# A two-layer hybrid decoder on one core: copies of late weights queued behind other ScalarE work, and a convolution spread over 25 weight units

## The chip, the core and the metric

The kernel runs on one core of a Trainium2 chip. TensorE (PE) multiplies, VectorE (DVE) and ScalarE (ACT) do elementwise work, GpSimd (POOL) here only raises a variance to the power -1/2, and SyncE (SP) issues the weight loads. The metric is the device time of one execution in microseconds, the median of the runs. The weight loads of PE, which overlap its matmuls, are called PEld.

## What is computed

Two layers over 256 rows of 1024 columns, all in fp32. Cut to what matters:

```python
for l in range(DEPTH):                                  # DEPTH = 2
    u = x * (1.0 + sc1) + sh1                           # sc, sh, gt: from c @ w_ada[l] + b_ada[l]
    proj = u @ w_in[l]                                  # q, k, v | GLU input | two gates
    attn = softmax(rope(q) @ rope(k).T / 8, causal) @ v # 8 heads of 64
    h = a * sigmoid(g)                                  # (a, g) = GLU input
    h = depthwise_conv(h, 31 taps) + b                  # along the 256 rows
    conv = silu(layer_norm(h))
    y = (sigmoid(g1) * (attn @ w_attn_br) + sigmoid(g2) * (conv @ w_conv_pw)) @ w_out
    x = layer_norm(ALPHA * x + (1.0 + gt1) * y)
    u = x * (1.0 + sc2) + sh2
    x = layer_norm(ALPHA * x + (1.0 + gt2) * (square(relu(u @ w_up)) @ w_down))
```

## The kernel before

Every fp32 matrix is split into a high part and a low part, and a product is three matmuls: high by high, high by low, low by high (`rowmm`, L317; `colmm`, L323). Weights come as 232 **units** of 128x1024 numbers in the order in which PE uses them. `Stream.make` (L114) does a unit: SP loads the raw unit `w`, ACT copies it into the high part `wh` (L122), DVE subtracts to get the low part `wl` (L123). The raw ring has 5 buffers, the split ring `RING` = 8: unit n+8 can be copied only after PE's last matmul on unit n. Units 0 to 115 belong to layer 1, 116 to 231 to layer 2. Of layer 2: 116 to 123 are the GLU input, 124 to 131 q and k, 132 to 135 v, 136 to 151 the gates (four groups g of four units), 152 to 155 the attention branch, 156 to 159 the convolution branch, 160 to 167 the output projection, 168 to 175 the first part of `w_up`.

A scheduler turns the program into one fixed queue per engine, and each engine takes its queue in that order. Beside PE's main stream, generators are advanced a step at each unit (`bg.step()`), so that their work falls between units: `conv_steps` (L595) yields `CONV_GAP[l]` units after each of its 60 tap steps; `attn_steps` (L647) runs scores (tile `s`), exponentials (`P`, L683, with sums `sm`), the scaling of `P` by 1/sum (L690), transposes (`ptr`, `PT`) and values (`av`, then `ah` and `al`) for four pairs of heads; `rope_steps` (L732) transposes q and k and copies them (`qT`, `kT`, L736); `ada_dve_gate` (L489) and `ada_dve_cols` (L463) accumulate the modulation on DVE (tile `adaa`).

At the end of each sub-layer the rows are normed in halves h = 0 and 1: `norm_half` (L547) on DVE (`ygt`, `xall`, `st`, `ag`, `ve`, then POOL's `rstd`, then `xall` again), and `make_u` (L526) per half and per c = 0, 1: PE transposes `xall` (tile `utr`), ACT makes `uf` (L535) and its high part `u` (L537), DVE its low part `u` (L538). The next sub-layer's matmuls read both parts of `u`. The convolution ends in `conv_steps` from L621: PE transposes `acc` (`ctr`), DVE norms (`cst`, `cag`, `ve`, `cn`), PE transposes back (`cbk`), ACT makes `cz`, a tanh and the high part `ch` (L643), DVE the low part `cl` (L644), per half. Units 156 to 159 multiply by `ch` and `cl`.

```python
a = nc.scalar.activation(wh, w, AF.Copy)                              # L122
b = nc.vector.tensor_tensor(wl, w, wh.bitcast(F32), op=ALU.subtract)  # L123
```

`order(later, earlier)` (L309) fixes that one instruction stands behind another in its engine's queue, without a wait.

Of the kernel before, what the change touches and what calls it, by code (L numbers as in the profile page):

```python
# [14 lines left out]
AF = mybir.ActivationFunctionType  # L15
# [10 lines left out]
HD = 64  # L26
# [8 lines left out]
RAW = 5  # L35
ADA_MIX = 2.0
ADA_BUFS = 3
CONV_GAP = (0.35, 0.35)
FIRST_AHEAD = 1
FIRST_ORDER = 8  # L40
FIRST_MM = 6
# [25 lines left out]
H = [slice(0, 128), slice(128, 256)]  # L67
# [33 lines left out]
class Stream:  # L101
# [3 lines left out]
    def __init__(self, nc, raw, split, units, order):  # L105
        self.nc, self.raw, self.split, self.units, self.order = nc, raw, split, units, order
        self.behind = ()
        self.splits = []
        self.after = None
        self.live = {}  # L110
        self.made = 0
        self.taken = 0

    def make(self):  # L114
        nc = self.nc
        src = self.units[self.made]
        w = self.raw.tile([128, 1024], F32, name=f"w{self.made}", tag="raw")
        v = w if len(src.shape) == 2 else w.rearrange("p (k n) -> p k n", k=src.shape[1])
        nc.sync.dma_start(v, src)
        wh = self.split.tile([128, 1024], F32R, name=f"wh{self.made}", tag="wh")  # L120
        wl = self.split.tile([128, 1024], F32R, name=f"wl{self.made}", tag="wl")
        a = nc.scalar.activation(wh, w, AF.Copy)  # L122
        b = nc.vector.tensor_tensor(wl, w, wh.bitcast(F32), op=ALU.subtract)  # L123
        for i, j in zip((a, b), self.behind):
            self.order(i, j)
        self.behind = ()
        if self.after is not None:
            self.order(b, self.after)
        self.splits.append(b)
        self.live[self.made] = (wh, wl)  # L130
        self.made += 1

# [21 lines left out]
def trunk_kernel(ctx: ExitStack, tc: tile.TileContext, x_in, c_in, positions, w_in, w_attn_br,  # L154
                 conv_dw_w, conv_dw_b, conv_ln_g, conv_ln_b, w_conv_pw, w_out, w_ada, b_ada,
                 ln_mix_g, ln_mix_b, w_up, w_down, ln_ffn_g, ln_ffn_b, out):
    nc = tc.nc
# [151 lines left out]
    def order(later, earlier):  # L309

        tc.add_manual_dep(later.ins, earlier.ins.name,
                          mybir.DependencyInfo(mybir.DependencyClass.NoSync, mybir.DependencyReason.DATA), reason="order")

    ws = Stream(nc, raw_p, split_p, units, order)
# [211 lines left out]
    def make_u(u, h, G, B, at):  # L526
        uh, ul, _ = u
        for c in range(2):
            ts = []
            b = transpose4(xt[h][:, 512 * c:512 * c + 512], "utr", ts)  # L530
            place(ts, at)
            f = t_p.tile([128, 4, 128], F32, name="uf", tag="t")
            for i in range(4):
                k = 4 * c + i
                nc.scalar.activation(f[:, i, :], b[:, 128 * i:128 * i + 128], AF.Identity, scale=G[:, k:k + 1], bias=B[:, k:k + 1])  # L535
            hi = uh[:, h, 4 * c:4 * c + 4, :]
            nc.scalar.activation(hi, f, AF.Copy)  # L537
            made_u[0] = nc.vector.tensor_tensor(ul[:, h, 4 * c:4 * c + 4, :], f, hi.bitcast(F32), op=ALU.subtract)  # L538

    def rstd_of(var, name):  # L540
        ve = s_p.tile([128, 1], F32, name="ve", tag="ve")
# [105 lines left out]
    def attn_steps(l, qkT, vs, hold):  # L647

        qT, kT = qkT
        ah = c_p.tile([128, 4, S], F32R, name="ah", tag="c")  # L650
        al = c_p.tile([128, 4, S], F32R, name="al", tag="c")
        hold["attn"] = (ah, al)
        sbs, Ps, sms, mxs, PTs = {}, {}, {}, {}, {}
        parts = (slice(0, 128), slice(128, 384))

        def scores(p):
            sb = []
            for e in range(2):
                es = slice(64 * e, 64 * e + 64)
                b = bank(f"s{e}")  # L660
                sb.append(b)
                nc.tensor.matmul(b[:, 0:128], qT[es, p, 0:128], kT[es, p, 0:128], start=True, stop=False, skip_group_check=True)
                nc.tensor.matmul(b[:, 128:384], qT[es, p, 128:256], kT[es, p, :], start=False, stop=False, skip_group_check=True)
            for e in range(2):
                nc.tensor.matmul(sb[e][:, 0:128], identb, maskb, start=False, stop=True, skip_group_check=True)
                nc.tensor.matmul(sb[e][:, 256:384], identb, maskb, start=False, stop=True, skip_group_check=True)
            mx = s_p.tile([128, 4], F32, name="mx", tag="mx")
            with tc.high_priority(MAX_PRIO):
                for e in range(2):
                    for i in range(2):  # L670
                        nc.vector.tensor_reduce(mx[:, 2 * e + i:2 * e + i + 1], sb[e][:, parts[i]], axis=AX.X, op=ALU.min)
            sbs[p], mxs[p] = sb, mx

        def exps(p):
            sm = s_p.tile([128, 4], F32, name="sm", tag="sm")
            Ps[p] = []
            for e in range(2):
                t = t_p.tile([128, 384], F32, name="P", tag="t")
                Ps[p].append(t)
                for i in range(2):  # L680
                    n = 2 * e + i
                    with tc.high_priority(EXP_PRIO):
                        nc.scalar.activation(t[:, parts[i]], sbs[p][e][:, parts[i]], AF.Exp, bias=mxs[p][:, n:n + 1],  # L683
                                             scale=-1.0, accum_out=sm[:, n:n + 1])
            with tc.high_priority(MAX_PRIO):
                nc.vector.reciprocal(sm, sm)
            for e in range(2):
                for i in range(2):
                    n = 2 * e + i
                    nc.scalar.activation(Ps[p][e][:, parts[i]], Ps[p][e][:, parts[i]], AF.Copy, scale=sm[:, n:n + 1])  # L690

        def transposes(p):
            PTs[p] = []
            for e in range(2):
                b = bank("ptr", tr)
                for i in range(3):
                    nc.tensor.transpose(b[:, 128 * i:128 * i + 128], Ps[p][e][:, 128 * i:128 * i + 128], ident)
                t = t_p.tile([128, 384], F32, name="PT", tag="t")
                with tc.high_priority(PT_PRIO):
                    nc.scalar.activation(t, b[:, 0:384], AF.Copy)  # L700
                PTs[p].append(t)

        def values(p):
            o = bank("av", tr)
            for e in range(2):
                es = slice(64 * e, 64 * e + 64)
                hs = slice((2 * p + e) * 64, (2 * p + e) * 64 + 64)
                nc.tensor.matmul(o[es, 0:256], vs[:, 0, hs], PTs[p][e][:, 0:256], start=True, stop=False, skip_group_check=True)
                nc.tensor.matmul(o[es, 128:256], vs[:, 1, hs], PTs[p][e][:, 256:384], start=False, stop=True, skip_group_check=True)
            hi = ah[:, p, :]  # L710
            nc.scalar.activation(hi, o[:, 0:256], AF.Copy)
            nc.vector.tensor_tensor(al[:, p, :], o[:, 0:256], hi.bitcast(F32), op=ALU.subtract)

        stages = (scores, exps, transposes, values)
        offs = ATTN_AT[l]
        for n in range(4 + offs[-1]):
            for k in reversed(range(len(stages))):
                if 0 <= n - offs[k] < 4:
                    stages[k](n - offs[k])
            yield ATTN_GAP[l]  # L720
# [11 lines left out]
    def rope_steps(l, qkt, qkT):  # L732
        for c in range(2):
            for h in range(2):
                b = transpose4(qkt[h][:, 512 * c:512 * c + 512], "qktr")
                nc.scalar.activation(qkT[c][:, :, H[h]], b.rearrange("p (q t) -> p q t", q=4), AF.Copy,  # L736
                                     scale=1.0 if c else -(HD ** -0.5))
            yield ROPE_GAP[l]

    def glu_gate(h, c, a, g):  # L740
# [257 lines left out]
    def relu2(src):  # L998
        r = t_p.tile([128, 512], F32, name="relu", tag="t")
        nc.scalar.activation(r, src, AF.Relu)  # L1000
        q = t_p.tile([128, 512], F32, name="relusq", tag="t")
        nc.scalar.activation(q, r, AF.Square)
        return q

    def relu2_wide(banks, hh, hl):

# [9 lines left out]
    def ffn(l, u):  # L1016
# [10 lines left out]
        for h in range(2):  # L1027
            b = [bank("u0"), bank("u1")]
            row_phase(ids, h, lhs, b, release=h == 1)
            for c in range(2):  # L1030
                q = relu2(b[c])
                ts = []
                tb = transpose4(q, "htr", ts).rearrange("p (f t) -> p f t", f=4)
                place(ts, HTR_AT[h][c])
                hh, hl = hid[c]
                nc.scalar.activation(hh[:, h], tb, AF.Copy)
                nc.vector.tensor_tensor(hl[:, h], tb, hh[:, h].bitcast(F32), op=ALU.subtract)
# [222 lines left out]
```

## Time and profile before

| | |
|---|---|
| time, median of 3 runs | 754.68 us (752.5 to 756.81) |
| the profiled execution's own time | 754.61 us |
| its span, first to last instruction | 752.5 us |
| busy: PE, PEld | 730.7 us (97%), 613.8 us (82%) |
| busy: DVE, ACT, POOL | 623.0 us (83%), 437.3 us (58%), 13.2 us (2%) |
| mean granted clock of PE | 0.995 of full speed |

Of the profiled execution's time 2.1 us lie outside its span. The end of a matmul is modelled, so busy time of PE says little; the distance from one matmul's start to the next says whether PE ran or waited. In the lists of waits a row names who waited for whom, with the sum, the count and the longest.

### The profile page before, as it was taken

Reading aid. Unit: us, or ns where it says so; the run is one execution under the profiler, and the core shown is the slowest. Engines: PE = TensorE matmul, PEld = TensorE weight load, DVE = VectorE, ACT = ScalarE, POOL = GpSimd, SP = SyncE. Lnnn points to the kernel's source line nnn. Section 1 sums busy time; section 2 is a strip of 40 time slices with the busy share of each in tenths; the row PEclk is TensorE's granted clock in tenths of the full one; section 3 lists DMA queues with packets and bytes.
Section 4 is the critical chain, followed back from the end, with each engine's and each line's share of the span. In section 5 each row is a group of like instructions: output and inputs, shape, how many; then the busy total and the mean of one; then the engine's idle time right before and its main releaser. Section 6 shows DMA issues by size and latency. Waiting matters only on the chain. (4 is left out here: it accounts for less than half of the span.)

```text
span 752.5 us, 11535 instructions
## 1 busy us (share of the span) xinstructions
PE 730.7 (97%) x4264; PEld 613.8 (82%) x4264; DVE 623.0 (83%) x942; ACT 437.3 (58%) x737; POOL 13.2 (2%) x37
## 2 busy tenths in 40 slices
PE   6999999999999999999999999999999999999995
PEld 4667788899888888888877888899988788888885
DVE  3448999999799999899899899998869895666657
ACT  4449898875575554544354875976447555454430
POOL 0000000010000000000000000001000000000001
PEclk9999999999999999999999999999999999999999
DMA  9999988677368999999786745436547896555501
GB/s 287 316 324 315 317 312 314 225 248 251 114 246 290 371 382 325 326 313 346 269 290 238 247 146 169 136 135 207 186 130 252 278 319 202 195 182 186 196 1 56
DMA packets 93847, 181.35 MB, mean 241 GB/s; under 512 B 6264, under 2 KB 49120, under 8 KB 93792
## 3 DMA queue, kind: packets, MB, share of 16 engines
q1 hardware_dynamic: 93728, 180.61, 70.9%
q8 instruction: 33, 0.54, 0.3%
q14 instruction: 22, 0.18, 0.1%
q10 hardware_dynamic: 64, 0.02, 0.0%
HBM read 179.56 MB, written 1.05 MB: 240 GB/s over the span
## 5 line engine op out<-in xcount | busy, mean ns | idle before, releaser
L122 ACT ACTIVATE wh<-w 128x1024 fp32r<-128x1024 f32 x232 | 243.0, 1059 | 170.1 <-issue 53.2
L123 DVE TENSOR_TENSOR wl<-w,wh 128x1024 fp32r<-128x1024 f32 x232 | 280.2, 1226 | 48.9 <-ACT wh L122 33.0
L319 PE MATMUL d<-wh,hh 128*128 128x512 f32 (+1 forms) x256 | 99.9, 390 | 0.0
L320 PE MATMUL d<-wl,hh 128*128 128x512 f32 (+1 forms) x256 | 99.0, 387 | 0.0
L321 PE MATMUL d<-wh,hl 128*128 128x512 f32 (+1 forms) x256 | 98.8, 386 | 0.0
L615 DVE SCALAR_TENSOR_TENSOR acc<-hconv,vc,acc 128x256 f32<-128x256 f32 x150 | 66.5, 507 | 0.0
L319 PEld LDWEIGHTS d<-wh,hh 128*128 128x128 f32 x256 | 48.2, 188 | 10.6 <-issue 0.8
L321 PEld LDWEIGHTS d<-wh,hl 128*128 128x128 f32 x256 | 48.1, 188 | 9.9
L320 PEld LDWEIGHTS d<-wl,hh 128*128 128x128 f32 x256 | 48.2, 188 | 8.7
L1055 PE MATMUL ub<-u,wh 128*128 128x512 f32 x192 | 48.1, 392 | 0.0
L1055 PE MATMUL ua<-u,wh 128*128 128x512 f32 x192 | 47.5, 389 | 0.0
L1055 PEld LDWEIGHTS ua<-u,wh 128*128 128x128 f32 x192 | 35.9, 188 | 7.4
L611 ACT ACTIVATE tap<-hconv,vc 128x256 f32<-128x256 f32 x90 | 39.4, 502 | 1.0 <-DVE qk L730 1.0
L1055 PEld LDWEIGHTS ub<-u,wh 128*128 128x128 f32 x192 | 34.5, 189 | 6.2
L500 DVE SCALAR_TENSOR_TENSOR adaa<-ada,ccol,adaa 128x1024 f32<-128x1024 f32 x28 | 35.9, 1281 | 3.8 <-DMA ada<-in_w_ada_dram 3.7
L325 PE MATMUL ga<-u,wh 128*128 128x256 f32 x128 | 37.5, 293 | 0.0
L325 PE MATMUL gb<-u,wh 128*128 128x256 f32 x128 | 36.9, 288 | 0.1
L326 PE MATMUL ga<-u,wh 128*128 128x256 f32 x128 | 36.8, 288 | 0.0
L327 PE MATMUL gb<-u,wl 128*128 128x256 f32 x128 | 36.4, 284 | 0.0
L326 PE MATMUL gb<-u,wh 128*128 128x256 f32 x128 | 36.3, 283 | 0.0
L327 PE MATMUL ga<-u,wl 128*128 128x256 f32 x128 | 36.2, 283 | 0.0
L473 DVE SCALAR_TENSOR_TENSOR adaa<-ada,ccol,adaa 128x1024 f32<-128x1024 f32 x28 | 35.8, 1282 | 0.3 <-DMA ada<-in_w_ada_dram 0.3
(271 smaller groups left out, 1544.4 us busy)
## 6 DMA issues: line engine op xcount, KB each, us to landing
ada<-in_w_ada_dram SPq DMA_DIRECT2D x80, 512.0 KB, 5.7
w<-in_w_in_dram SPq DMA_DIRECT2D x72, 512.0 KB, 5.4
w<-in_w_up_dram SPq DMA_DIRECT2D x64, 512.0 KB, 5.0
w<-in_w_down_dram SPq DMA_DIRECT2D x64, 512.0 KB, 4.4
ada<-in_w_ada_dram SPq DMA_DIRECT2D x32, 256.0 KB, 5.7
w<-in_w_out_dram SPq DMA_DIRECT2D x16, 512.0 KB, 3.3
w<-in_w_attn_br_dram SPq DMA_DIRECT2D x8, 512.0 KB
w<-in_w_conv_pw_dram SPq DMA_DIRECT2D x8, 512.0 KB, 4.2
```

Of the source, the lines that this page charges most:

```text
L122: a = nc.scalar.activation(wh, w, AF.Copy)
L123: b = nc.vector.tensor_tensor(wl, w, wh.bitcast(F32), op=ALU.subtract)
L319: nc.tensor.matmul(b, lh, wh, start=first, stop=False, skip_group_check=True)
L320: nc.tensor.matmul(b, lh, wl, start=False, stop=False, skip_group_check=True)
L321: return nc.tensor.matmul(b, ll, wh, start=False, stop=last, skip_group_check=True)
L325: nc.tensor.matmul(b, wh, rh, start=first, stop=False, skip_group_check=True)
L326: nc.tensor.matmul(b, wh, rl, start=False, stop=False, skip_group_check=True)
L327: nc.tensor.matmul(b, wl, rh, start=False, stop=last, skip_group_check=True)
L500: i = nc.vector.scalar_tensor_tensor(acc, src, ccol[:, j:j + 1], acc, op0=ALU.mult, op1=ALU.add)
L611: nc.scalar.activation(p[:, q % 2, :], hconv[:, q, j:j + S], AF.Copy, scale=w(j, q))
L615: nc.vector.scalar_tensor_tensor(acc[:, q, :], hconv[:, q, j:j + S], w(j, q), acc[:, q, :], op0=ALU.mult, op1=ALU.add)
L1055: nc.tensor.matmul(ub[f][:, 0:256 if s else 512], w, u2[:, k, 0:256 if s else 512], start=s == 0 and k == 0, stop=s == 1 and k == 7, skip_ ...
```

## The change

Four edits, all of them constants or orderings; no instruction is added or removed.

1. In `make_u` of half 0, the high copies of the third unit made after it and of all later ones, up to half 1's `make_u`, stand behind ACT's high part of `u`.
2. In `ffn`, the latest unit's copy emitted so far stands behind the last square of the relu.
3. In layer 2, the latest copies stand behind the scaled probabilities of a pair of heads, and behind the copies of q and of k.
4. `CONV_GAP` of layer 2 goes from 0.35 to 0.41 units a step: 60 steps take 24.6 units in place of 21.

```diff
-CONV_GAP = (0.35, 0.35)
+CONV_GAP = (0.35, 0.41)
...
+        if self.after_high is not None:
+            if self.made >= self.after_high[0]:
+                self.order(a, self.after_high[1])
         self.splits.append(b)
+        self.highs.append(a)
...
-            nc.scalar.activation(hi, f, AF.Copy)
+            made_hi = nc.scalar.activation(hi, f, AF.Copy)
...
+        ws.after_high = (ws.made + 3, made_hi) if h == 0 else None
...
+                    a = nc.scalar.activation(Ps[p][e][:, parts[i]], Ps[p][e][:, parts[i]], AF.Copy, scale=sm[:, n:n + 1])
+            if l:
+                order(ws.highs[-1], a)
...
+                i = nc.scalar.activation(qkT[c][:, :, H[h]], b.rearrange("p (q t) -> p q t", q=4), AF.Copy,
+                                         scale=1.0 if c else -(HD ** -0.5))
+            if l:
+                order(ws.highs[-1], i)
...
-                q = relu2(b[c])
+                q, sq = relu2(b[c])
+                if h == 1 and c == 1:
+                    order(ws.highs[-1], sq)
```

The scheduler builds all queues anew, so other engines move too. Line numbers of the changed kernel are up to 13 higher than before.

**DVE at the start of layer 1's channel mixer**, before. `o0`, `o1` are the output projection's banks of half 1, units 55 to 57 belong to `w_up`:

```order
L123 TENSOR_TENSOR wl55_2490<-w55_2487,wh55_2489 128x1024
L123 TENSOR_TENSOR wl56_2502<-w56_2499,wh56_2501 128x1024
L538 TENSOR_TENSOR u_2351<-uf_2424,u_2351 128x4x128
L553 TENSOR_TENSOR ygt_2542<-o0_2443,gt02_2328 128x512
L538 TENSOR_TENSOR u_2351<-uf_2436,u_2351 128x4x128
L557 BN_AGGR ag_2550<-st_2541 128x2
L542 TENSOR_SCALAR ve_2552<-ag_2550 128x1
L565 TENSOR_SCALAR xall_120<-xall_120,ag_2550,rstd_2554 128x512 x2
L123 TENSOR_TENSOR wl57_2514<-w57_2511,wh57_2513 128x1024
```

The same place with the change:

```order
L544 TENSOR_TENSOR u_2351<-uf_2424,u_2351 128x4x128
L561 TENSOR_TENSOR ygt_2542<-o0_2443,gt02_2328 128x512
L544 TENSOR_TENSOR u_2351<-uf_2436,u_2351 128x4x128
L563 BN_STATS st_2541<-xall_120 128x6 x2
L125 TENSOR_TENSOR wl55_2490<-w55_2487,wh55_2489 128x1024
L565 BN_AGGR ag_2550<-st_2541 128x2
L125 TENSOR_TENSOR wl56_2502<-w56_2499,wh56_2501 128x1024
L550 TENSOR_SCALAR ve_2552<-ag_2550 128x1
L573 TENSOR_SCALAR xall_120<-xall_120,ag_2550,rstd_2554 128x512 x2
L125 TENSOR_TENSOR wl57_2514<-w57_2511,wh57_2513 128x1024
```

The splits of units 55 and 56 have moved from ahead of half 0's low parts of `u` into half 1's norm, ahead of `ve`. The same happens in layer 2 (units 171 and 172). At the start of layer 2 itself, in the GLU input, the split of unit 119 moves in the same way, behind both low parts and the `st` of half 1, where the split of 120 and those behind it keep their places.

**ACT at the end of layer 2's convolution**, before. `cth_5626` and `ch_5497` are half 1's:

```order
L122 ACTIVATE wh159_5687<-w159_5685 128x1024
L640 ACTIVATE cth_5626<-cz_5621 128x512
L960 ACTIVATE gate_5691<-gb_5525 128x512
L122 ACTIVATE wh160_5722<-w160_5720 128x1024
L643 ACTIVATE ch_5497<-cth_5626 128x4x128
L122 ACTIVATE wh161_5752<-w161_5750 128x1024
L122 ACTIVATE wh162_5786<-w162_5784 128x1024
L122 ACTIVATE wh163_5816<-w163_5814 128x1024
```

With the change:

```order
L124 ACTIVATE wh160_5677<-w160_5675 128x1024
L645 ACTIVATE cz_5686<-cbk_5681,vh1_2326 128x128 x4
L648 ACTIVATE cth_5691<-cz_5686 128x512
L651 ACTIVATE ch_5629<-cth_5691 128x4x128
L124 ACTIVATE wh161_5737<-w161_5735 128x1024
L645 ACTIVATE cz_5746<-cbk_5741,vh1_2326 128x128 x4
L124 ACTIVATE wh162_5786<-w162_5784 128x1024
L648 ACTIVATE cth_5751<-cz_5746 128x512
L124 ACTIVATE wh163_5816<-w163_5814 128x1024
L651 ACTIVATE ch_5629<-cth_5751 128x4x128
```

The high part of half 1 stood behind the copy of unit 160 and stands now behind that of unit 163. On DVE its low part stands behind the two merges of the attention branch (`gate`, L977) and the split of 163. On PE the `ctr` of half 0 moves from unit 148 to the end of 151, the last `cbk` from 151 to the middle of 154; four matmuls on the high part of units 156 and 158 stand ahead of the first one that needs the low part.

**ACT at layer 2's q and k**, with the change (`vs` is v's half 1; before, the copy of 144 stood between `vs` and `qT`, that of 145 between `qT` and `kT`):

```order
L958 ACTIVATE vs_4318<-v1_4745 128x512
L746 ACTIVATE qT_4844<-qktr_4884 128x4x128
L124 ACTIVATE wh144_4874<-w144_4872 128x1024
L746 ACTIVATE kT_4845<-qktr_4932 128x4x128
L124 ACTIVATE wh145_4922<-w145_4920 128x1024
L691 ACTIVATE P_5036,sm_5035<-s0_4946,mx_4956 128x128
```

The two copies of 144 and 145 now follow what they stood ahead of. Further on PE the transposes of the third pair of heads' `P` move from unit 147 to 145, those of the fourth from 148 to 146.

## Rows read from the trace of the kernel before

**Rows 1.** The page's part 1: busy time of each engine over the span.

```profile
PE 730.7 (97%) x4264; PEld 613.8 (82%) x4264; DVE 623.0 (83%) x942; ACT 437.3 (58%) x737; POOL 13.2 (2%) x37
```

**Rows 2.** Waits of PE: who for whom, sum in us, times, longest.

```profile
PE glu L321 <- DVE u L538: 1.2, 1, 1.2
PE s L662 <- ACT kT L736: 0.9, 1, 0.9
PE htr L373 <- ACT relusq L1002: 0.7, 1, 0.7
PE ptr L697 <- ACT P L690: 0.5, 1, 0.5
PE glu L320 <- DVE wl L123: 0.5, 1, 0.5
PE glu L319 <- ACT u L537: 0.4, 1, 0.4
```

**Rows 3.** Windows: us, busy of PE, PEld, DVE, ACT, POOL, granted clock, DMA.

```profile
393.90:397.20 3.30, 3.30 (x9) 2.62 (x8) 3.30 (x7) 2.12 (x2) 0.00 (x0) 0.50 0.94 338
455.00:477.00 22.00, 20.22 (x170) 18.00 (x169) 22.00 (x46) 14.51 (x30) 0.00 (x0) 1.00 0.49 149
```

**Rows 4.** Timeline of PE, layer 2's start: start, us, what, [idle before, releaser].

```profile
389.90 0.39 PE L320 MATMUL d<-wl,hh 128*128 128x512 f32 x1
390.13 0.39 PE L321 MATMUL d<-wh,hl 128*128 128x512 f32 x1
390.89 0.50 PE L319 MATMUL glu<-wh,u 128*128 128x512 f32 x1 [0.38 <-ACT u L537]
...
392.80 0.50 PE L321 MATMUL glu<-wh,u 128*128 128x512 f32 x1 [1.17 <-DVE u L538]
...
393.90 0.63 PE L319 MATMUL glu<-wh,u 128*128 128x512 f32 x1
...
397.26 0.40 PE L321 MATMUL glu<-wh,u 128*128 128x512 f32 x1
```

**Rows 5.** Timeline of DVE at the same place.

```profile
390.92 1.22 DVE L123 TENSOR_TENSOR wl<-w,wh 128x1024 fp32r<-128x1024 f32 x1
392.06 0.69 DVE L538 TENSOR_TENSOR u<-uf,u 128x512 fp32r<-128x512 f32 x1
...
401.03 1.00 DVE L565 TENSOR_SCALAR xall<-xall,ag,rstd 128x512 f32<-128x512 f32 x2 [0.44 <-POOL rstd L544]
```

**Rows 6.** Timeline of DVE, start of layer 1's channel mixer.

```profile
200.99 4.63 DVE L123 TENSOR_TENSOR wl<-w,wh 128x1024 fp32r<-128x1024 f32 x4
205.53 0.69 DVE L538 TENSOR_TENSOR u<-uf,u 128x512 fp32r<-128x512 f32 x1
...
210.82 0.15 DVE L542 TENSOR_SCALAR ve<-ag 128x1 f32<-128x1 f32 x1
...
212.56 3.49 DVE L123 TENSOR_TENSOR wl<-w,wh 128x1024 fp32r<-128x1024 f32 x3
```

**Rows 7.** Timelines of ACT and PE there: half 0's high part, unit 57's low product.

```profile
204.40 0.65 ACT L537 ACTIVATE u<-uf 128x512 fp32r<-128x512 f32 x1
214.26 0.40 PE L320 MATMUL u<-wl,u 128*128 128x512 f32 x1
```

**Rows 8.** Timeline of ACT, layer 2's q and k: the copies of units 144 and 145.

```profile
458.10 1.06 ACT L122 ACTIVATE wh<-w 128x1024 fp32r<-128x1024 f32 x1 [1.77 <-DMA w<-in_w_in_dram]
459.07 1.06 ACT L736 ACTIVATE qT<-qktr 128x512 f32<-128x512 f32 x2
460.76 1.06 ACT L122 ACTIVATE wh<-w 128x1024 fp32r<-128x1024 f32 x1 [0.63 <-DMA w<-in_w_in_dram]
```

**Rows 9.** Timelines at the end of the convolution: DVE, ACT, then PE and ACT.

```profile
515.55 0.81 DVE L632 TENSOR_SCALAR cn<-ctr,cag,rstd 128x512 f32<-128x512 f32 x1 [0.73 <-POOL rstd L544]
522.29 0.65 ACT L643 ACTIVATE ch<-cth 128x512 fp32r<-128x512 f32 x1
523.60 0.68 DVE L644 TENSOR_TENSOR cl<-cth,ch 128x512 fp32r<-128x512 f32 x1
529.44 0.28 PE L325 MATMUL ya<-ch,wh 128*128 128x256 f32 x1
529.52 1.06 ACT L122 ACTIVATE wh<-w 128x1024 fp32r<-128x1024 f32 x1 [1.82 <-PE yb L326]
```

More of the change, by code (lines that the diff above doesn't have):

```diff
@@ L108, in __init__ @@
         self.splits = []
+        self.highs = []
         self.after = None
+        self.after_high = None
         self.live = {}
@@ L689, in exps @@
                     n = 2 * e + i
-                    nc.scalar.activation(Ps[p][e][:, parts[i]], Ps[p][e][:, parts[i]], AF.Copy, scale=sm[:, n:n + 1])
+                    a = nc.scalar.activation(Ps[p][e][:, parts[i]], Ps[p][e][:, parts[i]], AF.Copy, scale=sm[:, n:n + 1])
+            if l:
+                order(ws.highs[-1], a)
         def transposes(p):
@@ L735, in rope_steps @@
                 b = transpose4(qkt[h][:, 512 * c:512 * c + 512], "qktr")
-                nc.scalar.activation(qkT[c][:, :, H[h]], b.rearrange("p (q t) -> p q t", q=4), AF.Copy,
-                                     scale=1.0 if c else -(HD ** -0.5))
+                i = nc.scalar.activation(qkT[c][:, :, H[h]], b.rearrange("p (q t) -> p q t", q=4), AF.Copy,
+                                         scale=1.0 if c else -(HD ** -0.5))
+            if l:
+                order(ws.highs[-1], i)
             yield ROPE_GAP[l]
@@ L1001, in relu2 @@
         q = t_p.tile([128, 512], F32, name="relusq", tag="t")
-        nc.scalar.activation(q, r, AF.Square)
-        return q
+        return q, nc.scalar.activation(q, r, AF.Square)
     def relu2_wide(banks, hh, hl):
```

## Prediction

> **What bounds the kernel now.** I read the busy times first. PE is busy for 97% of the span, DVE for 83%, ACT for 58% [rows 1]. So time is won only where PE waits or runs at its lower clock, and lost where a moved instruction makes PE wait. The list of PE's waits comes next. Those that this change touches are 1.2, 0.5 and 0.4 us at the start of layer 2 (its GLU input), 0.9 and 0.5 us in attention, and 0.7 us at the relu [rows 2]: 4.2 us together. The timelines then show what each place costs.
>
> At layer 2's start PE's matmuls are 0.23 us apart while it runs freely (389.90, 390.13). The next start is 390.89, which is 0.53 us later than that, and the start at 392.80 is two pitches after 390.89, so 1.91 - 0.46 = 1.45 us late [rows 4]: 2.0 us are lost. After that come 8 pitches from 393.90 to 397.26, 3.36 us in place of 8 x 0.23 = 1.84 [rows 4], with a granted clock of 0.50, the lower level of 1.2 GHz [rows 3]. That costs 1.5 us more. DVE is what PE waits for here: it goes from a split of 1.22 us straight to the low part of u [rows 5], and is busy for all of 393.90 to 397.20, as it is for all 22 us of attention from 455 to 477 [rows 3]. Thus nothing can be moved to DVE's front at these places without another thing going back.
>
> The sum below is made against the profiled execution: 754.61 us, of which 752.5 are its span and 2.1 lie around it. The median is 0.07 us above it. A measurement of this kernel tells about 0.5% from no change, 3.8 us: under 750.9 is faster, over 758.45 slower.
>
> **The change part by part.** Nothing is added or removed, so each price is a wait that goes or comes.
>
> *Start of the channel mixer, twice.* Before, DVE does four splits from 200.99 and then, at 205.53, the low part of u: 4.54 / 4 = 1.14 us a split [rows 6]. ACT had the high part at 204.40 + 0.65 = 205.05 [rows 7]. With the change units 55 and 56 are split later, so DVE waits until 205.05 and makes the low part 0.48 us sooner, but does two splits, 2.27 us, ahead of half 1's `ve`, which goes 1.8 us later. Everything behind it is delayed by the same: POOL's `rstd`, both `xall`, and the split of unit 57. That one started at 212.56 [rows 6], took 1.22 us [rows 5] to 213.78, and PE used it at 214.26 [rows 7], with 0.5 us to spare. It would end at 215.6, where PE wants it at some 214.5, as the second high product can stand ahead of it (one pitch). I take 1.0 us each, **+2.0**. The low end is 0 each, if half 1's norm has idle time into which both splits fit. The high end is the whole shift of 1.8 each, if half 1's transposes, which wait for `xall`, hold PE too.
>
> *Start of layer 2.* Here the split of 119 goes behind the low parts, so that the low part of u can come 1.14 us sooner, and ACT's copy no longer stands before the high part. This attacks the 0.53 and 1.45 us. But DVE has no idle time until 401.03, where it waits 0.44 us for POOL [rows 5]. The split of 119 goes back by the low parts, the `ygt` and the `st` that now precede it, while those of 120 and 121 keep their places. PE, which reaches them 1.5 us sooner, finds them missing. The wait moves from u to `wl`. I take **-0.2**. The low end is -3.5 (2.0 of waits and 1.5 of clock), the high end +0.5, as large as the wait for `wl` that is already there [rows 2].
>
> *The relu's squares.* A copy of a late unit no longer stands ahead of the square that PE's transposes `htr` wait for. That copy is wanted many units later, so the 0.7 us [rows 2] go: **-0.7**, and nothing is late in its place.
>
> *Attention.* Before, the copy of 144 waited 1.77 us for its DMA, that of 145 0.63 us, with `qT` and then `kT` behind them on ACT [rows 8]. Now they follow. That bounds the gain: the waits for `kT` and `P` are 0.9 and 0.5 us [rows 2], and qktr can win up to about 0.5 more, so -1.9. But `P` is scaled by 1/sum from DVE, which has no idle time here [rows 3], and PE takes the third and fourth pairs' transposes two units sooner; DVE is then waited for instead. I leave 0.4 us of the wait for `kT` and 0.3 us at the transposes: **-1.2**. High end +0.5, if the wait of the fourth pair is again as long as the longest for `P`.
>
> *End of the convolution.* Before, `ch` of half 1 started at 522.29 and `cl` was done at 523.60 + 0.68 = 524.28; PE's first matmul on unit 156 came at 529.44, 5.2 us later [rows 9]. Spare, that is. The copy that started at 529.52, after waiting 1.82 us for PE [rows 9], is that of unit 163: it must wait for PE's end of unit 155, as the ring has 8. With the change `ch` of half 1 stands behind this very copy. Let X be the time at which PE has finished 155, just when it wants `ch`. The copy starts at X + 0.08 and takes 1.06 us, `ch` takes 0.65: X + 1.8. On DVE `cl` stands behind two gate merges and the split of 163, itself waiting for that copy: X + 0.08 + 1.06 + 1.22 = X + 2.4, then 0.68 for `cl`, X + 3.05. The four high products that PE does first save about 4 x 0.12 = 0.5 us, with the pitch halved for 256 columns. Stall: 2.6 us. Besides, DVE's norm of half 0 (`ctr` to `cbk`) now runs between units 151 and 154: split 1.22, POOL 0.73, `cn` 0.81 [rows 5, 9] and about 1.6 for small steps are 4.4 us, where PE has some 3.7 us of other work; 0.7, and as half 1's chain is the same but starts sooner against PE, 0.5. Sum **+3.8**. The low end is 2.0 (the merges and the split done sooner: X + 1.8 + 0.68 - 0.5, and both chains covered), the high end 5 (the four matmuls save nothing and each chain is 0.35 longer). No gain can stand here, as nothing waited.
>
> The spread of the taps, 24.6 units in place of 21, adds no time on DVE; it frees DVE earlier and loads it later, and its price is the lost 5.2 us.
>
> Sum: 2.0 - 0.2 - 0.7 - 1.2 + 3.8 = **+3.7 us**, 754.6 + 3.7 = **758.3 us**, 0.5% above before. If the terms err independently (their distances to the ends squared and added), it lies between 754.0 and 761.0.
>
> Two rules speak to this. DVE stays full at layer 2's start, so a wait removed there comes back under another name [rows 3, 5]. The Trainium skill ("Perfetto Trace Analysis", Optimization Strategy) says to find the gaps on the engine that is contended most and to make what ends them come sooner; the change does that, and by it alone the time would be the faster rival's below. The clock fell to 0.50 after PE's gaps at 390 to 393, yet stayed at 1.00 with those of attention [rows 3]. The Trainium skill ("Perfetto Trace Analysis", Matmul Optimizations) says that matmuls should run back to back, as power follows use; by that the new gap at unit 156 would cost clock as well. The trace agrees at the one place and not at the other.
>
> **The rivals.** *Faster:* the waits of [rows 2] go and nothing takes their place. Then 2.0 + 1.5 at layer 2's start, 1.9 in attention and 0.7 at the relu are 6.1 us, and with the end of the convolution between nothing and its low end of 2.0 the time is 748.5 to 750.5. It decides whether DVE has free time between 390 and 401. For it speaks that ACT, 58% busy [rows 1], has room for every copy that is put off. Against it speaks that DVE has none there [rows 3, 5].
>
> *They cancel:* every term but layer 2's start is at its low end: 0 - 0.2 - 0.7 - 1.9 + 2.0 = -0.8, so 753.8; halfway from there to the forecast 756. For it: half 1's norm may well wait for PE, as the page's DVE share of 83% leaves time somewhere [rows 1]. Against: unit 57 had only 0.5 us to spare.
>
> *Slower by the clock:* the gap at unit 156 is some 2.6 us, longer than the two at layer 2's start, which were followed by half clock [rows 3, 4]. As there, 1.5 us more: 759.8, and up to 761.5 with the mixer's waits near their high end. [...]
>
> *The orders do nothing:* each binds only the latest copy emitted, so earlier and later ones might slip around it. The built queues show the copies moved at all these places, so I give this no chance of its own.
>
> **How the numbers follow.** The forecast, 0.47: 758.3 lies 0.15 under the bound of slower, so 0.27 of it fall to the same and 0.20 to slower. Cancelling, 0.23, all the same. The clock, 0.17, all slower. Faster, 0.13. That makes faster 0.13, same 0.27 + 0.23 = 0.50, slower 0.20 + 0.17 = 0.37. The range goes from 752.5, under the cancelling case, to 761.5, the top of the clock's; outside it lie the faster rival and a rest of some 0.05.
>
> **What would show it.** In the changed kernel's profile PE should wait some 2.6 us at unit 156 for DVE's `cl` or ACT's `ch`, and about 1 us for `wl` at the third unit of each channel mixer. The wait of `htr` for the squares should be gone and that of `s` for `kT` halved. At layer 2's start the waits for u should give way to waits for the splits of 119 to 121, and a window of half clock may stand there still. I am wrong if PE comes to unit 156 without a wait (then `ch` did not hang on the copy of 163), if layer 2's start shows neither waits nor half clock (then DVE had time), or if PE's other stretches change their length.

## The result, and the profile after

The changed kernel takes 758.33 us (median of 16 runs, 756.3 to 760.73) against 753.58 us for the kernel before (16 runs). The ratio is 1.0061, with a 95% interval of 1.0049 to 1.0074: 3.7 to 5.6 us slower. The profiled execution took 757.3 us, 755.4 of them in its span, which is 2.9 us more than the span before.

The page's part 1 hardly differs from [rows 1]: the same work is done.

```profile
PE 731.4 (97%) x4264; PEld 613.1 (81%) x4264; DVE 622.3 (82%) x942; ACT 435.6 (58%) x737; POOL 12.3 (2%) x37
```

The list of PE's waits is another one than in [rows 2]. Those for `kT` and `P` have left it, and four of the nine rows below belong to the end of the convolution (`ya` and `cbk`, 3.2 us). Layer 2's start no longer waits for u, but for weights.

```profile
PE glu L326 <- DVE wl L125: 3.0, 3, 1.2
...
PE ya L331 <- ACT ch L651: 1.6, 1, 1.6
PE u L326 <- DVE wl L125: 0.8, 2, 0.4
PE ya L332 <- DVE cl L652: 0.7, 1, 0.7
PE ptr L707 <- DVE al L722: 0.6, 1, 0.6
PE cbk L379 <- DVE cn L640: 0.6, 1, 0.6
...
PE cbk L379 <- ACT wh L124: 0.3, 1, 0.3
PE htr L379 <- ACT relusq L1014: 0.3, 1, 0.3
PE utr L379 <- DVE xall L573: 0.2, 1, 0.2
```

The costliest place is unit 156, in the timelines of PE, ACT and DVE of the changed kernel. These rows answer to [rows 9].

```profile
528.98 0.28 PE L333 MATMUL yb<-ah,wl 128*128 128x256 f32 x1
530.81 0.39 PE L331 MATMUL ya<-ch,wh 128*128 128x256 f32 x1 [1.55 <-ACT ch L651]
...
531.27 0.28 PE L331 MATMUL yb<-ch,wh 128*128 128x256 f32 x1
532.30 0.38 PE L332 MATMUL ya<-cl,wh 128*128 128x256 f32 x1 [0.75 <-DVE cl L652]
...
529.18 1.06 ACT L124 ACTIVATE wh<-w 128x1024 fp32r<-128x1024 f32 x1 [1.22 <-PE yb L332]
530.15 0.61 ACT L651 ACTIVATE ch<-cth 128x512 fp32r<-128x512 f32 x1
...
530.42 1.22 DVE L125 TENSOR_TENSOR wl<-w,wh 128x1024 fp32r<-128x1024 f32 x1
531.56 0.68 DVE L652 TENSOR_TENSOR cl<-cth,ch 128x512 fp32r<-128x512 f32 x1
```

PE ends unit 155 with the start at 528.98. That releases the copy of unit 163 on ACT at 529.18. Only behind it comes `ch` at 530.15, and PE goes on at 530.81, 1.7 us after the 0.12 us of an undisturbed pitch. Then DVE splits unit 163 (530.42) and makes `cl` behind it (531.56); PE, whose four high products began at 530.81 to 531.27, loses 0.9 us more. Nothing here is slow: every instruction takes what it took before, and stands behind another one.

To see where the rest went I measure each stage by the starts of PE's first matmuls on named tiles, in the profiled executions. M1 and M2 are the channel mixers up to the down projection (first `u` to first `d`), S1 layer 2's start up to the values (first `utr` to first `v`), S2 attention, gates and branches (first `v` to first `o`). Below, a "late start" is what the distance between two starts has over the pitch that this form of matmul has while PE runs freely.

| | M1 | S1 | S2 | M2 |
|---|---|---|---|---|
| before | 23.63 | 55.73 | 99.17 | 23.75 |
| the change | 24.72 | 54.80 | 101.51 | 24.80 |
| difference | +1.09 | -0.93 | +2.34 | +1.05 |

These make +3.6 us; of the rest of the span's +2.9, 0.4 us were won ahead of M1, where PE's queue is the same, and 0.7 us at layer 2's relu, less 0.4 lost at layer 1's.

A warning on single profiles: PE's queue up to M1 is the same in all fourteen of them (the kernel before, the change and the experiments below), and yet M1 begins between 205.7 and 209.5 us. A stage can be compared from one profile to the next; a whole span only to some 4 us.

### The profile page after: what moved, and what is told of

Read it like the earlier page. It is cut to its first block, busy times and chain, and to the rows that moved or that the text cites. A ratio compares the mean times of both kernels' runs of the same rounds, so it can differ in the third digit from the quotient of the medians.

```text
span 755.4 us, 11540 instructions
## 1 busy us (share of the span) xinstructions
PE 731.4 (97%) x4264; PEld 613.1 (81%) x4264; DVE 622.3 (82%) x942; ACT 435.6 (58%) x737; POOL 12.3 (2%) x37
## 3 DMA queue, kind: packets, MB, share of 16 engines
HBM read 179.56 MB, written 1.05 MB: 239 GB/s over the span
## 5 line engine op out<-in xcount | busy, mean ns | idle before, releaser
L623 DVE SCALAR_TENSOR_TENSOR acc<-hconv,vc,acc 128x256 f32<-128x256 f32 x150 | 64.8, 474 | 0.0
```

Of the source, the lines that this page charges most:

```text
L623: nc.vector.scalar_tensor_tensor(acc[:, q, :], hconv[:, q, j:j + S], w(j, q), acc[:, q, :], op0=ALU.mult, op1=ALU.add)
```

## The experiments

Each time stands against the kernel before, measured beside it. The mean clock is PE's granted clock averaged over the timed runs; that of before is 0.9965 or 0.9966 beside each experiment. As an estimate, 0.001 less is worth at most 0.75 us, since 1.5 of 750 us at half the speed cost that much where PE is never idle. The stages are those of the one profiled execution of each.

| | kernel | us (runs) | before | ratio, interval | clock | M1 | S1 | S2 | M2 |
|---|---|---|---|---|---|---|---|---|---|
| | the change | 758.33 (16) | 753.58 | 1.0061, 1.0049 to 1.0074 | 0.9962 | 24.72 | 54.80 | 101.51 | 24.80 |
| 1 | spread 0.41 alone | 758.35 (12) | 753.56 | 1.0060, 1.0038 to 1.0082 | 0.9941 | 23.70 | 54.58 | 100.75 | 23.63 |
| 2 | all orders, spread 0.35 | 759.91 (6) | 753.56 | 1.0070, 1.0043 to 1.0097 | 0.9937 | 24.78 | 54.73 | 105.69 | 24.78 |
| 3 | orders but the mixers', 0.35 | 756.73 (12) | 753.56 | 1.0033, 1.0015 to 1.0051 | 0.9929 | 23.64 | 54.47 | 101.41 | 23.70 |
| 4 | the change, `ch` first | 756.87 (12) | 753.56 | 1.0031, 1.0013 to 1.0049 | 0.9971 | 24.78 | 55.21 | 98.94 | 24.80 |
| 5 | spread 0.41, `ch` first | 753.87 (12) | 753.94 | 0.9995, 0.9977 to 1.0013 | 0.9966 | 23.64 | 55.15 | 99.25 | 23.63 |
| 6 | spread 0.38 alone | 752.99 (12) | 753.94 | 0.9990, 0.9973 to 1.0006 | 0.9967 | 23.65 | 54.81 | 98.82 | 23.63 |
| 7 | u orders, mixers only | 757.91 (12) | 753.94 | 1.0046, 1.0026 to 1.0067 | 0.9965 | 24.77 | 55.03 | 98.79 | 24.80 |
| 8 | P, q, k orders only | 758.27 (12) | 753.94 | 1.0050, 1.0028 to 1.0072 | 0.9921 | 23.63 | 56.02 | 103.01 | 23.59 |
| 9 | 0.38, `ch` first, late adaa | 752.16 (12) | 754.07 | 0.9967, 0.9949 to 0.9986 | 0.9952 | 23.63 | 53.50 | 99.05 | 23.63 |
| 10 | 0.38, q and k orders | 753.17 (12) | 754.07 | 0.9991, 0.9971 to 1.0011 | 0.9967 | 23.64 | 54.99 | 98.82 | 23.63 |
| 11 | as 1, again | 755.44 (10) | 754.07 | 1.0025, 1.0007 to 1.0044 | 0.9950 | 23.59 | 54.90 | 101.42 | 23.63 |
| 12 | 5 and all orders but the mixers' | 753.32 (12) | 754.20 | 0.9987, 0.9971 to 1.0003 | 0.9948 | 23.64 | 55.04 | 99.06 | 23.63 |

### 1. The spread alone

```diff
 (the kernel before)
-CONV_GAP = (0.35, 0.35)
+CONV_GAP = (0.35, 0.41)
```

> Before with CONV_GAP 0.41 and no order. Theory: the wait at the end of the convolution comes from the spread of the taps alone, since the built ACT order has the high part of half 1 behind the copy of 163 here too. PE waits 0.8 and 0.5 us for cbk, 1.7 us for ch and 0.9 us for cl, 3.8 us in all; attention keeps its waits of before (2.6 us of late starts between 459 and 475). Time about 753.6 + 3.8 = 757.4 us. Rival: the loss comes from the orders: within 0.5 us of 753.6. Second rival: the gain in attention is the spread's doing (fewer taps on DVE there): attention's late starts fall to about 1.1 us, time about 756.

The end of the convolution lost the same 3.8 us as in the change, so it is the spread's doing, as the theory said. But the second rival was right as well: attention's late starts are nearly gone without any order. Of 2.6 us between 459 and 475 before, 0.4 are left. This row of the windows answers to the second one of [rows 3]: PE is busy for 21.90 us of 22 in place of 20.22, with DVE full in both.

```profile
455.00:477.00 22.00, 21.90 (x189) 20.21 (x188) 22.00 (x48) 15.43 (x39) 0.00 (x0) 1.00 0.56 165
```

The timelines of DVE tell why; first this experiment's row for the minima of the first pair's scores (tile `mx`), then two of the kernel before.

```profile
462.78 0.81 DVE L678 TENSOR_REDUCE mx<-s 128x1 f32<-128x128 f32 x3
```

```profile
467.09 1.71 DVE L615 SCALAR_TENSOR_TENSOR acc<-hconv,vc,acc 128x256 f32<-128x256 f32 x4
468.67 0.33 DVE L671 TENSOR_REDUCE mx<-s 128x1 f32<-128x128 f32 x1
```

Before, DVE had taps of the convolution to do first, and the minima came at 468.67. With the taps spread over more units they came at 462.78, and only then can ACT begin the exponentials (S2 itself begins 1.0 us sooner in this profile, so 4.9 of these 5.9 us are won within it). The late start at `s` went as well, though the copies of 144 and 145 still stand ahead of `qT` and `kT`. The load of 144 needs the raw buffer that DVE's split of 139 frees, and that split comes 3.9 us sooner too. The timelines of DVE and SP, before:

```profile
453.28 1.25 DVE L123 TENSOR_TENSOR wl<-w,wh 128x1024 fp32r<-128x1024 f32 x1
454.60 0.37 SPq L119 DMA_DIRECT2D w<-in_w_in_dram  x1
```

and here, with ACT's copy of 144, which no longer waits for its load:

```profile
449.36 1.22 DVE L125 TENSOR_TENSOR wl<-w,wh 128x1024 fp32r<-128x1024 f32 x1
450.64 0.37 SPq L121 DMA_DIRECT2D w<-in_w_in_dram  x1
454.73 1.06 ACT L124 ACTIVATE wh<-w 128x1024 fp32r<-128x1024 f32 x1 [1.21 <-PE gb L332]
```

So the DMA that `kT` waited for before [rows 8] was itself late for DVE. In its profile this kernel thus loses 3.8 and wins 2.2 us, +1.6 in S2. The median of 758.35 is higher than that. The profiled execution was the fastest of the twelve (754.6 us), and the mean clock over the runs is 0.0025 lower than before, worth 1.9 us at most; experiment 11 takes this up.

### 2. All orders, without the spread

```diff
 (the change)
-CONV_GAP = (0.35, 0.41)
+CONV_GAP = (0.35, 0.35)
```

> The change with CONV_GAP back at 0.35, all orders kept. Theory: the 3.8 us at the end of the convolution go and the rest stays: 758.3 - 3.8 = 754.5 us, with PE waiting 0.8 us in each channel mixer and 3.4 us at layer 2's start. Rival (the gain in attention is the spread's doing): attention's late starts return, 1.4 us more, 755.9 us.

Both were wrong, and in the same direction: the waits for `ch` and `cl` are gone, and yet the kernel is no faster than the change. PE now waits 2.5 us for `P` in attention, the granted clock is 0.50 for 6.8 us behind that, and at the end of the convolution one `cbk` starts 2.1 us late, which neither expectation had; S2 takes 105.69 us. The orders alone are no gain; with DVE as full as before they are a loss.

### 3. The orders without those of the mixers

```diff
 (experiment 2)
-        ws.after_high = (ws.made + 3, made_hi) if h == 0 else None
+        ws.after_high = (ws.made + 3, made_hi) if h == 0 and late else None
...
-                if h == 1 and c == 1:
+                if l and h == 1 and c == 1:
```

`late` is true for layer 2's start alone.

> CONV_GAP 0.35, no order behind u in the channel mixers, the order behind the squares in layer 2 alone; kept are the orders behind u at layer 2's start, behind P, q, k, and behind layer 2's squares. Theory: the parts add up, -0.9 at layer 2's start, -1.4 in attention, -0.7 at the relu: 753.6 - 3.0 = 750.6 us. Rival: attention's gain needs the spread: 752.0 us. Rival: the parts do not add, since the late splits at layer 2's start only pass their wait on: 752.9 us or more.

The first two did not hold: 756.73 us, 3.2 us above before. The third allowed for it (752.9 or more), but not for the reason it gave, as S1 is 1.3 us shorter than before and the loss is in S2, +2.2 us. The mixers are back at 23.6 us, so their loss was the orders'. PE waits 1.3 us for `P` in one piece, behind which the clock is 0.50 for 3.4 us, and 2.4 us for `wl` at layer 2's start; the mean clock is 0.9929.

### 4. The change with `ch` first

```diff
-            nc.scalar.activation(hi, th, AF.Copy)
-            nc.vector.tensor_tensor(cl[:, :, H[h]], th, hi.bitcast(F32), op=ALU.subtract)
+            i = nc.scalar.activation(hi, th, AF.Copy)
+            j = nc.vector.tensor_tensor(cl[:, :, H[h]], th, hi.bitcast(F32), op=ALU.subtract)
+            if l and h == 1:
+                order(ws.highs[-1], i)
+                order(ws.splits[-1], j)
```

> The change, and besides the copy and the split of 163 stand behind the high and the low part of the convolution's half 1. Theory: ch and cl are late only for the copy of 163, so PE's waits of 1.7 and 0.9 us at unit 156 fall to 0.5 us in all; the waits for cbk, 0.8 and 0.5 us, stay. Time about 758.3 - 2.1 = 756.2 us. Rival: the whole chain of the convolution is late by the spread itself, so PE waits 1.5 us or more at unit 156 for ch or cl without the copy ahead of them; time 757.2 us or more.

The waits at unit 156 went altogether, 2.6 us. The waits for `cbk` stayed, 1.2 us of late starts at 521.95 and 527.25 in its trace. S2 fell from 101.51 to 98.94. So `ch` and `cl` were late for the copy and the split of 163 alone. The time is 1.5 us under the change's, somewhat less than the trace wins.

### 5. The spread with `ch` first, no other order

```diff
 (experiment 1, and the edit of experiment 4)
```

> Before with CONV_GAP 0.41, and the copy and split of 163 behind the high and low part of the convolution's half 1; none of the change's orders. Theory now: the spread takes taps from DVE in attention, so that the row minima of the scores come sooner, worth 2.2 us there, and costs 3.8 at the end of the convolution, of which 2.6 hang on the copy of 163. Those go: 753.6 - 2.2 + 1.2 = 752.6 us. Rival: typical runs with the spread have more time at half clock than the profiled one (mean clock 0.994 against 0.997 of before, 1.9 us): 754.5 us.

It lies between the two, at the time of before; the clock of the rival did not show (0.9966). Against experiment 4, whose only difference are the orders, S2 is the same within 0.3 us and the mixers are 1.1 us shorter each.

### 6. Half the spread

```diff
 (the kernel before)
-CONV_GAP = (0.35, 0.35)
+CONV_GAP = (0.35, 0.38)
```

> Before with CONV_GAP 0.38, no order. Theory now: in the built order ch of half 1 stands ahead of the copy of 161 again and the two norms have two units each, so the end of the convolution costs at most 0.5 us; the pairs' transposes stand where they do with 0.41 up to the third pair, so attention wins most of its 2.2 us: 752.0 us. Rival: half the spread frees half the time on DVE, the minima come too late and the third pair's transposes wait: 753.6 us or more.

The trace follows the theory in kind, not in size: the end of the convolution costs 0.9 us (two late starts of `cbk`; at most 0.5 were expected), none at unit 156, and in attention 1.5 of 2.6 us are left, where most of 2.2 us were to go. The time is 0.9 us below before, which the interval does not tell from no change.

### 7. The orders of the channel mixers alone

```diff
 (the kernel before, with the Stream and make_u parts of the change; late is true in the mixers alone)
+        ws.after_high = (ws.made + 3, made_hi) if h == 0 and late else None
```

> Before with the order behind u in both channel mixers alone. Theory: 1.05 us in each mixer, 753.6 + 2.1 = 755.7 us; in layer 1's relu no wait, if the order behind the squares made it, else 0.4 us more. Rival: half 1's norm has idle time for both splits: 753.6 us.

The theory's size was low: 757.91 us, 4.0 us above before (2.0 to 5.1 by the interval). M1 and M2 are 1.1 us longer each, as expected. Besides, `htr` starts 0.6 us late in layer 1 and 0.7 in layer 2, in two pieces each, where experiments 1, 5 and 6 have about 0.2 at most. In the change, which also has the order behind the squares, they are 0.4 and 0.15 us. Set against experiments 1, 5 and 6, the trace thus makes some 3 us of the 4.0.

### 8. The orders behind P, q and k alone

```diff
 (the kernel before)
+            if l:
+                order(ws.highs[-1], a)
...
+            if l:
+                order(ws.highs[-1], i)
```

> Before with the orders behind P, q and k alone, CONV_GAP 0.35. Theory now: kT comes 0.8 us sooner, but DVE is as full as before, so the sums and with them P are late where PE now wants its transposes sooner: a wait of 1.3 to 2.5 us for P at about 472 and some microseconds of half clock behind it as in the runs with CONV_GAP 0.35 before; 755.5 to 757.0 us. Rival, the prediction's own: -1.2 us, 752.4 us.

The new theory held in kind, and the upper end of its range was passed: 758.27 us. This experiment goes most clearly against the prediction's term for attention. First the rows of the kernel before (timelines of PE and ACT), then those of this one (PE, ACT and DVE; then a row of its windows, whose clock is the third number from the end):

```profile
474.91 0.33 PE L697 MATMUL ptr<-ident,P 128*128 128x128 f32 x1 [0.51 <-ACT P L690]
...
474.47 1.48 ACT L690 ACTIVATE P<-P,sm 128x128 f32<-128x128 f32 x4
```

```profile
474.77 0.33 PE L706 MATMUL ptr<-ident,P 128*128 128x128 f32 x1 [1.44 <-ACT P L697]
...
474.32 1.49 ACT L697 ACTIVATE P<-P,sm 128x128 f32<-128x128 f32 x4 [1.42 <-DVE sm L693]
...
468.95 0.28 DVE L678 TENSOR_REDUCE mx<-s 128x1 f32<-128x128 f32 x1
```

```profile
475.30:482.10 6.80, 6.80 (x30) 5.53 (x30) 6.19 (x17) 5.80 (x19) 0.00 (x0) 0.50 0.40 122
```

The minima come at 468.95 (before: 468.67), and so `P` is scaled at 474.32 (474.47), with ACT idle ahead of it; PE's transposes of the first pair start at 474.77 (474.91). S2 begins 0.7 us later in this profile; counted from its start, PE comes to the scores `s` 1.8 us sooner than before, but the minima come only 0.4 us sooner. What the orders win at `kT` PE thus waits for later, nearly all of it: late starts of 0.41, 1.08, 0.68 and two of about 0.2 us have become two of 0.2 and one of 1.6. And this one long wait is followed by 6.8 us at the lower clock level, 1.2 GHz, which costs 3.4 us; before, the clock stayed at 1.00 here [rows 3]. Where the clock fell is known for the profiled execution alone, but the mean clocks of all twelve runs are low, 0.988 to 0.994. And the profiles of experiments 2 and 3, which have the same orders and the same spread, show 0.50 at the same place, for 6.8 us from 475.3 and 3.4 us from 475.9. The Trainium skill ("Perfetto Trace Analysis", Matmul Optimizations) says that matmuls should be issued back to back, since the engine's power follows its use; the trace agrees at this place, and that of the change does not at unit 156, where the clock stays at 1.00 behind 2.6 us of waits.

### 9. Less on DVE at layer 2's start

```diff
 (the kernel before, CONV_GAP 0.38, the edit of experiment 4, and in ada_dve_gate)
                 if ws.after is not None:
                     order(i, ws.after)
+                if (l, v) == (1, 2) and j > 3:
+                    order(i, made_u[0])
-            yield gap or ADA_FFN
+            yield 10.0 if (l, v, j) == (1, 2, 3) else gap or ADA_FFN
```

> Before with CONV_GAP 0.38, the copy and split of 163 behind ch and cl, and four of the eight additions of the modulation of layer 2's mixer (tile adaa, 1.28 us of DVE each) put off until DVE has made half 1's u. Theory: layer 2's start waits for a full DVE, so orders on ACT can't help there, and 5.1 us less on DVE can: PE's late starts between 390 and 406 fall from 3.3 us in the run with CONV_GAP 0.38 to under 1.2; attention as there or up to 0.7 worse, as taps start no sooner; 753.0 - 2.0 = 751.0 us. Rival: the bound there is the chain from the norm over POOL and the transposes, not DVE's load: late starts stay over 2.5 us, 753 us.

In the changed kernel DVE's timeline at this place has three additions of the modulation between the weights' splits and the norm that PE waits for, each 1.2 to 1.3 us of DVE, and PE's timeline three waits for `wl`:

```profile
390.02 1.28 DVE L506 SCALAR_TENSOR_TENSOR adaa<-ada,ccol,adaa 128x1024 f32<-128x1024 f32 x1
...
397.26 1.23 DVE L506 SCALAR_TENSOR_TENSOR adaa<-ada,ccol,adaa 128x1024 f32<-128x1024 f32 x1
...
401.05 1.28 DVE L506 SCALAR_TENSOR_TENSOR adaa<-ada,ccol,adaa 128x1024 f32<-128x1024 f32 x1
...
397.27 0.50 PE L326 MATMUL glu<-wl,u 128*128 128x512 f32 x1 [0.95 <-DVE wl L125]
...
399.74 0.50 PE L326 MATMUL glu<-wl,u 128*128 128x512 f32 x1 [0.81 <-DVE wl L125]
...
403.51 0.50 PE L326 MATMUL glu<-wl,u 128*128 128x512 f32 x1 [1.21 <-DVE wl L125]
```

With these put off, one wait of 0.82 us is left there (late starts of about 1 us, where under 1.2 were expected), and two new ones of about 0.5 us come where the additions went (timeline of PE, this experiment):

```profile
394.98 0.50 PE L327 MATMUL glu<-wh,u 128*128 128x512 f32 x1 [0.82 <-DVE u L546]
...
423.00 0.44 PE L759 MATMUL gtr<-ident,gth 128*128 128x128 f32 x2 [0.57 <-DVE gth L756]
...
425.08 0.50 PE L456 MATMUL gtb<-gh,ones 128*128 128x512 f32 x1 [0.48 <-ACT hconv L760]
```

S1 is 1.3 us shorter than in experiment 6, the shortest of all. The time, 752.16 us, is 1.9 us below before (1.1 to 3.8 us by the interval). The only new thing against experiment 6 that touches S1 is work taken from DVE. In time the two are not clearly apart: their intervals overlap, and it is S1 that tells them apart.

### 10. Half the spread, and the orders behind q and k

```diff
 (experiment 6)
+            if l:
+                order(ws.highs[-1], i)
```

> Before with CONV_GAP 0.38 and the orders behind q and k alone. Theory: with DVE relieved a kT that comes sooner is worth its wait: the late start at s falls from 0.87 to 0.2 us and nothing takes its place; 753.0 - 0.7 = 752.3 us. Rival: as with the orders at CONV_GAP 0.35, the wait is only passed on to the transposes of P, in one piece: 753.0 us, or 755 and more if half clock follows.

The rival: the late start at `s` fell from 0.87 to 0.17 us, one of 0.63 us for `P` has come in its place, and S2 is the same to a hundredth, 98.82 us. No half clock followed, and the time did not change.

### 11. The first experiment again

> The first experiment once more (CONV_GAP 0.41, no order), for a second profile, as its profiled execution was the fastest of 12 and had no half clock outside the end. Theory: the spread's extra loss over its waits is half clock that follows one of PE's waits: behind the 2.6 us at unit 156, or at layer 2's start; mean clock about 0.994, time about 758 us. Rival: the loss is in the waits alone, and the first run's slower executions were a matter of its chip: mean clock 0.997, about 755 us.

It answers half of the question. The waits are those of experiment 1 again (1.6 and 0.7 us at unit 156, 0.9 for `cbk`), and S2 is 2.25 us longer than before; the time, 755.44 us, is 1.4 us above before, about what the waits make. The profile's granted clock is at its lower level from 14.2 to 17.5 us, in the setup, and at the end of the span, not behind unit 156. One late start is there that the profile of experiment 1 lacks, 0.75 us at 490.44, where the transposes wait for `al`; the change and experiments 4, 5 and 12 have it too. Why the twelve runs of experiment 1 took 2.9 us longer stays open; both together put the price of the spread alone at 0.5 to 6 us (the intervals' ends), and the traces at 1.6 to 2.3.

### 12. All orders but the mixers', on the fifth experiment

```diff
 (experiment 5, with the change's orders except those of both mixers and of layer 1's squares)
```

> The fifth experiment (CONV_GAP 0.41, the copy and split of 163 behind ch and cl) and besides the change's other orders: behind u at layer 2's start, behind P, q and k, and behind layer 2's squares; those of the channel mixers and of layer 1's squares are left out. Theory: given the spread these orders win nothing, as DVE sets the waits at each of their places: 753.9 us as without them, within 1 us, and layer 2's start loses 3.3 us as before. Rival, the prediction's terms: -0.2, -1.2 and -0.7 us, 751.8 us.

The theory: 753.32 us against 753.87 of experiment 5. S1 is 0.1 and S2 0.2 us shorter. So once the taps are spread, the orders behind u at layer 2's start, behind P, q and k, and behind the squares win nothing that can be told from nothing.

## Why the prediction was right, and where its reasons were not

The time of 758.3 us was met, and so were the place and the size of the largest term. That it was met to a tenth of a microsecond is luck: the sum was made against 754.6 us, the median of 16 runs before is 753.58, and the difference is 4.75 us where +3.7 stood. Of the five terms two, the relu and attention, had about the right size for a wrong reason, and one step failed outright.

- **End of the convolution, +3.8.** Right, term by term. The trace shows 1.7 and 0.9 us at unit 156 (2.6 expected) and late starts of 0.8 and 0.5 us at the two `cbk` (0.7 and 0.5 expected): 3.8 us. Experiment 1 shows that the spread makes them, experiment 4 that `ch` and `cl` hung on the copy and split of unit 163.
- **Channel mixers, +2.0.** The size was right: M1 and M2 are 1.09 and 1.05 us longer. The place was half right. I had all of it at the split of unit 57. The rows of the changed kernel's DVE and PE at M1 show that PE already waits for the split of 55 (0.5 us late), which now follows half 1's `st`, and then 0.3 us late at `utr` for `xall`, behind the `ve` that came at 212.12; unit 57, from 213.85 on, was in time:

```profile
204.72 0.69 DVE L544 TENSOR_TENSOR u<-uf,u 128x512 fp32r<-128x512 f32 x1 [1.74 <-ACT u L543]
...
209.79 1.21 DVE L125 TENSOR_TENSOR wl<-w,wh 128x1024 fp32r<-128x1024 f32 x1
...
212.12 0.14 DVE L550 TENSOR_SCALAR ve<-ag 128x1 f32<-128x1 f32 x1
...
213.85 2.35 DVE L125 TENSOR_TENSOR wl<-w,wh 128x1024 fp32r<-128x1024 f32 x2
...
211.05 0.50 PE L326 MATMUL u<-wl,u 128*128 128x512 f32 x1 [0.38 <-DVE wl L125]
...
213.53 1.11 PE L379 MATMUL utr<-ident,xall 128*128 128x128 f32 x8
```

  DVE's idle 1.74 us ahead of 204.72 are where the two splits stood before. Experiment 7 shows a wait of `htr` besides, which the prediction had not seen.
- **Layer 2's start, -0.2.** The mechanism held: the waits for u gave way to waits for the splits, as DVE stayed full. But the -0.9 of S1 is not the orders' gain: the profile of before held the half clock of [rows 3], 1.5 us, and that of the change did not; set against a before without it, S1 would be 0.6 us longer. Experiments with this order have an S1 of 54.5 to 55.2 us, those without it (9 apart) 54.6 to 56.0; experiments 5 and 12, which differ by all the orders but the mixers', are 0.1 apart. So no gain is shown here, and none of -0.2 could be.
- **Relu, -0.7.** The wait went, but not because of the order: it is 0.2 in experiments 1, 5 and 6 too, which have none there. It was an accident of the one execution that I read. The timeline of ACT before shows why; below it is that of experiment 11, with the same instructions in the same order:

```profile
589.21 0.63 ACT L1002 ACTIVATE relusq<-relu 128x512 f32<-128x512 f32 x1
590.53 1.06 ACT L122 ACTIVATE wh<-w 128x1024 fp32r<-128x1024 f32 x1 [0.68 <-DMA w<-in_w_down_dram]
```

```profile
590.46 0.64 ACT L1009 ACTIVATE relusq<-relu 128x512 f32<-128x512 f32 x1
591.00 1.04 ACT L124 ACTIVATE wh<-w 128x1024 fp32r<-128x1024 f32 x1
```

  The copy between the two squares waited 0.68 us for a load that in the other execution had landed. A wait for a DMA that is seen once is not a term of a sum.
- **Attention, -1.2.** About 1.5 us were won in the change's trace, late starts of 2.6 us having become 0.3 and a new one of 0.8 at 491.53, but the orders did not win them. The spread did (experiment 1). The step that failed is the sentence on the spread, that it "adds no time on DVE", frees it earlier and loads it later, and that "its price is the lost 5.2 us". I had read that DVE was full from 455 to 477 [rows 3], and that its sums therefore set `P`; I had not drawn from it that fewer taps there are a gain, 2.2 us in the trace of experiment 1, in which the minima and the splits that free the raw buffers both come sooner. With DVE as full as before the orders cost 4.3 us (experiment 8), of which the trace puts 3.4 down to half clock.

So, by the traces, the change is the sum of a spread that loses 3.8 and wins 2.2 us, of mixer orders that lose 2.1 us in M1 and M2 and 0.4 at layer 1's `htr`, and of other orders that win nothing once the spread is there: 1.6 + 2.5 = 4.1 us, where 3.7 to 5.6 were measured. The times add up less well: 4.8 us for the spread alone (1.4 when it was measured again) and 4.0 for the mixers' orders alone make 8.8 or 5.4 us, so the places are shown, and the sizes only to within a few microseconds. The rival by clock is not needed: the mean clock of the change's runs is 0.9962, against 0.9966 of before beside the first experiments, worth 0.3 us at most, and its trace has no half clock behind unit 156.

## What to carry to other kernels

In this kernel, where the engine that PE waits for was full, reordering another engine's queue moved the wait and hardly shortened it; in a like place, look for work on the full engine itself that can be put elsewhere, as the taps in attention and the modulation's additions at layer 2's start. A producer must not stand in a queue behind an instruction that waits for the consumer's own progress: here a weight copy that the ring released only when PE had come to the point where it wanted `ch`. And before a wait for a DMA goes into a forecast, see whether a second execution shows it.

## What was not expected of the hardware

At one place the clock cost more than the waits. One wait of 1.6 us in attention was followed by 6.8 us at 0.50 in experiment 8, and those of 2.5 and 1.3 us at the same place in experiments 2 and 3 by 6.8 and 3.4 us, where waits of a larger sum, 2.6 us in five pieces, left it at 1.00 before. Yet the 1.7 and 0.9 us at unit 156 show no such stretch in any of the three profiles that have them (the change, 1 and 11), and the waits at layer 2's start show one in the kernel before and in none of the others here. The profile of experiment 9 has 3.4 us at 0.50 from 125.0 us on, at the end of a wait of PE's of 2.5 us for a load, in a part of layer 1 where its queues are those of before. So the length of the one wait alone does not decide it, and what does, these runs leave open.
